# A hybrid encoder layer on one core: the far stretch's stores on GpSimd's queue, eight tiles for the last value chunks, vectors and memory loaded elsewhere

## The chip, the cores and the metric

The kernel runs on one core of a Trainium2 chip. The metric is the device time of one execution in microseconds (us), smaller is better. A core has TensorE (PE in the profile; PEld is its weight load), VectorE (DVE), ScalarE (ACT), GpSimd (POOL) and SyncE (SP). A transfer is issued by an engine: it stands in that engine's queue in program order, behind whatever that engine waits for, and then runs on the core's 16 DMA engines.

## The reference

One transformer layer on x of 2048 rows by 1024 columns, with 256 rows of memory:

```
h = x + W_out [ DilatedSWA(q,k,v) || ConformerConv(u) ],  (q,k,v,u) = RMSNorm(x) W_in
h = h + CrossAttn(RMSNorm(h), RMSNorm(mem))
h = h + SqReLU-MLP(RMSNorm(h)),   then a last RMSNorm
```

DilatedSWA is attention over three banded patterns (dilation 1, 4 and 16), whose three outputs are combined for each head by a softmax over their log-denominators. The convolution has 31 taps. The cross attention's keys and values are products of the 256 memory rows with w_xk and w_xv; the kernel multiplies the values further with w_xo (a quarter of the heads at a time) before it uses them.

## The kernel before, in words

Every large product is made of three matmuls: both factors are split into a high and a low part, and `mm3` (L263, L264, L265) adds high*high, low*high and high*low. So each weight chunk is loaded (a tile `raw`), its high part is cast by ACT (`whi`, L254), and its low part is a subtraction on DVE or POOL (`wlo`, L255; `lwlo`, L221).

The order of the program is written as Python generators that are woven into each other (`weave`), with helpers that pin a stream behind an engine's last instruction (`pinned`, `behind`), and a scheduler in the tile framework then lays the rows out for each engine. `dma` (L57) issues on SP's queue unless a queue is named. Tiles of one tag are buffers that are taken in turn: a writer of a tile waits until the reader of what lay there before is done.

By the trace, the stages are these. **Start** (0 to some 140 us): `setup` (L154) loads seven gain vectors and the convolution's weights `cwn` from ACT's queue, transposes them on PE into the bank `pvec` and makes `gv`, `cw` and `gmix`; `xprep` (L388 to L408) loads four blocks of x (`xn`), sums squares on ACT (`junk`, L375), transposes on PE (`xt`, L400), scales on DVE (`xv`, L405) and splits on ACT and POOL (`xh`, `xl`); `glu_first` is the first projection. `memory` (L414) loads and normalises the memory rows behind `xprep` 3. **Projections** to some 420 us. **Far stretch** (420 to 690): attention of the first quarter of rows, and woven into it the rest of the gated projections and the class `Matrices`: `proj` (keys and values of the memory), `turn` (transposed w_xq chunks, `xqt`, L523), `score` (`pa`, `ea`). All of these write results to scratch in DRAM on SP's queue: `pscr` (`kscr`/`vscr`<-`ve`), `uscr`, `ascr`. SP's queue carries the attention's own loads too (`k`, `qh`, `ql`, `v`, and `ld`, which is read back from `oscr`).

`combine` (L1061) joins the three patterns for two heads: it loads `ld` (SP), takes a minimum `csm` on DVE (L1081, L1082), works on POOL (L1083 to L1109) to `cat`, which PE transposes (`catT`, L1117). Its `yield`s say how many attention units lie between the steps.

**Backs** (690 to 746): `Matrices.back(i)` for i = 24 to 31 multiplies values with a chunk of w_xo (`raw_m24` to `raw_m31`, 512 KB each): for each i, two banks `pb` of six matmuls of 512 columns, each emptied by ACT into a tile `eb` (L563, through two tiles of the tag `ve`) and stored to `bscr` on SP. The chunks have two tiles `raw`, loaded two ahead on POOL's queue; `load_cat` puts 14 transfers of 256 KB (`cath`, `catl`) on SP just before. **w_out** and the rest (MLP and so on) run from 746 to the end; its first chunks `raw_o` are loaded by `ahead`.

Of the kernel before, what the change touches and what calls it, by code (L numbers as in the profile page):

```python
# [10 lines left out]
F32 = mybir.dt.float32  # L11
# [10 lines left out]
P = 128  # L22
# [25 lines left out]
def hybrid_layer(ctx, tc, A, out):  # L48
# [103 lines left out]
    cst.tile([P, 8], F32, name="lpad")  # L152
    lin = ExitStack()
    def setup():  # L154
        vecs, cwn = t2("vecs", F32, (64, P)), t2("cwn", F32, (32, DCONV))
        DVE.memset(vecs, 0.0)
        DVE.memset(cwn, 0.0)
        for nm, key in (("norm_mix_g", "mix"), ("norm_x_g", "x"), ("norm_mlp_g", "mlp"),
                        ("conv_b", "conv_b"), ("conv_ln_g", "ln_g"), ("conv_ln_b", "ln_b")):
            v = A[nm][0].rearrange("(k p) -> k p", p=P)  # L160
            dma(vecs[GV[key]:GV[key] + v.shape[0], :], v, nc.scalar)
        dma(vecs[GV["final"]:GV["final"] + 8, :], A["norm_final_g"].rearrange("(k p) -> k p", p=P), nc.scalar)
        dma(cwn[0:CW, :], A["conv_w"][0], nc.scalar)
        pv = ps("c", "pvec")
        PE.transpose(pv[:, 0:64], vecs, ident[0:64, 0:64])
        for c in range(4):
            PE.transpose(pv[:, 64 + 32 * c:96 + 32 * c], cwn[:, c * P:(c + 1) * P], ident[0:32, 0:32])
        ACT.copy(gv, pv[:, 0:64])
        ACT.activation(cw.rearrange("p a b -> p (a b)"), pv[:, 64:192], AF.Copy, scale=0.5)
# [11 lines left out]
        DVE.tensor_scalar(gmix, g8, top_[:, 4:5], None, op0=ALU.mult)  # L181

    def pow2_scale(c, inv, v, t, bits=0):

# [259 lines left out]
    class Matrices:  # L444
# [6 lines left out]
            self.split(0)  # L451

        def load(self, i):
            if i >= 32:
                return
            raw = wp.tile([P, 8, P] if i < 24 else [P, 2, 512], F32, tag="raw", name=f"raw_m{i}", bufs=2)
            if i < 24:
                src = wcols((w_xk, w_xv, w_xq)[i // KC], i % KC * P)
            else:
                h, nh = divmod(i - 24, 2)  # L460
                src = w_xo[256 * h:256 * h + 256, 512 * nh:512 * nh + 512].rearrange("(e p) m -> p e m", p=P)
            dma(raw, src, nc.gpsimd)
            self.ring[i] = raw
# [26 lines left out]
        def proj(self, i):  # L490
            mq = self.mq
            x, j = "kv"[i // KC], i % KC
            self.load(i + 2)
            wh, wl = self.ring.pop(i)
            pt = ps("mm", f"px{x}{j}")[:, 0:NMEM]
            for k in range(KC):
                mm3(pt, wh[:, k, :], wl[:, k, :], mq[k // 4][:, k % 4, :], mq[2 + k // 4][:, k % 4, :],
                    k == 0, k == KC - 1)
                if k == 1 and i + 1 < 16:
                    self.split(i + 1)  # L500
                if k % 2 and k < KC - 1:
# [3 lines left out]
            ACT.copy(t[0], pt)  # L505
            DVE.tensor_tensor(t[1], pt, f(t[0]), op=ALU.subtract)
            for q in range(2):
                dma(f(pscr[x][q, j]), f(t[q]))
            if i == 15:
                self.kt = [self.gather("k", h) for h in range(XH)]  # L510
                self.vt = []
            yield
# [19 lines left out]
        def score(self, h):  # L532
            kt, wt = self.kt, self.wt
            for k2 in range(4):
                pt = ps("mm", f"pa{h}{k2}")
                for q in range(2):
                    k = 2 * k2 + q
                    for e in range(2):
# [3 lines left out]
                e3 = ev.rearrange("p (q m) -> p q m", q=2)  # L542
                DVE.tensor_tensor(e3, pt.rearrange("p (q m) -> p q m", q=2),
                                  self.rbm.unsqueeze(1).to_broadcast([P, 2, NMEM]), op=ALU.mult)
                dma(ascr[h // 2, :, 2 * k2:2 * k2 + 2, h % 2, :], e3)
                if k2 == 3:
                    self.vt.append(self.gather("v", h))
                yield

        def back(self, i):  # L550
            h, nh = divmod(i - 24, 2)
            self.load(i + 2)
            wh, wl = self.ring.pop(i)
            vt = self.vt
            for mc in range(2):
                ms = slice(mc * P, (mc + 1) * P)
                pt = ps("mm", f"pb{h}{nh}{mc}")
                for e in range(2):
                    mm3(pt, vt[h][:, 0, e, ms], vt[h][:, 1, e, ms], wh[:, e], wl[:, e], e == 0, e == 1)
                if mc == 0:  # L560
                    self.split(i + 1)
                ev = f(self.pl.tile([P, 512], F32R, tag="ve", name=f"eb{h}{mc}{nh}", bufs=2))
                ACT.activation(ev, pt, AF.Copy, scale=rmem[:, mc:mc + 1])  # L563
                dma(bscr[4 * nh:4 * nh + 4, :, 2 * h + mc, :].rearrange("m p c -> p m c"),
                    ev.rearrange("p (m c) -> p m c", c=P))
                yield

    def linear(wh, wl, n):
# [31 lines left out]
    def glu(c, ns, fine=False):  # L600
# [4 lines left out]
        def unit(x, c0):  # L605
# [10 lines left out]
            for n in ns:  # L616
# [7 lines left out]
                else:  # L624
                    u = t2(f"u{c}_{n}")
                    last["dve"] = DVE.scalar_tensor_tensor(u, sig[n], 1.0, pt, op0=ALU.add, op1=ALU.mult)
                    dma(uscr[c][:, 15 + 512 * n:15 + 512 * (n + 1)], u)
                yield

        return unit("g", 3 * DATT + DCONV + c * P), unit("a", 3 * DATT + c * P)  # L630
# [271 lines left out]
    with ExitStack() as st:  # L902
# [7 lines left out]
        next(x1)  # L910
        next(four)
        next(four)
        next(x0)
        for _ in range(3):
            behind("sumsq", four)
        drain(x0)
        for _ in range(3):
            behind("x0_3", four)
        behind("x0_5", x1)
# [371 lines left out]
    with ExitStack() as st:  # L1291
# [6 lines left out]
        def filler():  # L1298
# [10 lines left out]
            mats.split(24)  # L1309
            yield from gated  # L1310

        rest = pinned(filler(), "pe")
        for _ in range(30):
            next(rest)
# [28 lines left out]
        def backs():  # L1343
            for i in range(24, 32):
                yield from mats.back(i)
            yield from pipeline(ahead(0), ahead(1))

        weave(pinned(backs(), "pe"), (first, 0.55))


    banks.update(mm=(0, 1, 2), O=(7,))
# [635 lines left out]
```

## Time and profile before

| | us |
|---|---|
| three runs: median, lowest, highest | 2821.86, 2818.76, 2829.14 |
| the profiled execution | 2827.31 |
| its span in the trace | 2825.5 |
| PE busy, DVE busy, ACT busy, POOL busy | 2697.4, 1898.2, 1272.6, 525.7 |

A row of a timeline shows the start, the duration, the engine, the line, the operation with the tile written and the tiles read, and in square brackets how long the engine had been idle and who released it. "issue" there means that the engine waited for nothing that the profile shows. A row of the waits shows engine, line, releaser, total us, times and the longest. A row of a window shows its length, then each engine's busy time with its number of instructions, the granted PE clock, the share of the DMA engines and GB/s.

### The profile page before, as it was taken

The numbers are of one execution on the slowest core, as the hardware profiler recorded it, in microseconds if no ns is written. First come the engines' busy times: TensorE is split into PE (matmuls) and PEld (weight loads), VectorE is DVE, ScalarE is ACT, GpSimd is POOL, SyncE is SP. The second block draws the span as 40 slices with busy tenths as digits, with TensorE's granted clock in tenths as the row PEclk, the third lists the DMA queues.
The fourth block names the chain that finished last, engine by engine and source line by source line (L and its number), as shares of the span: only waits on it lengthen the run. The fifth ranks groups of instructions, "written<-read, shape, count | busy, mean of one in ns | idle before, by whom it ended". The sixth has DMA issues, their size and how long they took to land.

```text
span 2825.5 us, 40587 instructions
## 1 busy us (share of the span) xinstructions
PE 2697.4 (95%) x14783; PEld 2075.6 (73%) x14783; DVE 1898.2 (67%) x3475; ACT 1272.6 (45%) x2171; POOL 525.7 (19%) x716
## 2 busy tenths in 40 slices
PE   6999999988899999999999999999999999999998
PEld 3544447775687787788788888887887788878887
DVE  4468826654589876668987478766475776566765
ACT  5742216644444434434554444454344444444434
POOL 4454402321002122300211201121010122100000
PEclk9999999999899999999999999999999999999999
DMA  8765547876834666776457867774534554584553
GB/s 257 204 179 117 137 133 194 256 209 190 239 114 157 214 212 211 243 226 214 144 170 227 267 190 223 239 236 141 175 122 131 182 191 156 181 292 155 166 183 104
DMA packets 484257, 535.69 MB, mean 190 GB/s; under 512 B 98021, under 2 KB 357721, under 8 KB 484056
## 3 DMA queue, kind: packets, MB, share of 16 engines
q1 hardware_dynamic: 452176, 427.76, 50.8%
q0 software_dynamic: 30032, 101.99, 10.2%
q10 hardware_dynamic: 1848, 3.33, 0.3%
q8 instruction: 116, 1.90, 0.3%
q14 instruction: 85, 0.70, 0.1%
HBM read 384.46 MB, written 148.52 MB: 189 GB/s over the span
## 4 chain that ended last, share of the span: by engine, by line
PE 69%; DMA 9%; issue 8%; DVE 6%; ACT 4%; POOL 2%; SPq 1%; ACTq 0%; POOLq 0%; DVEq 0%
PE b L1685 7%; PE dn L263 4%; PE dn L264 4%; PE dn L265 4%; PE up L263 3%; PE up L265 3%; PE up L264 3%; PE lin L263 2%; PE lin L265 2%; PE lin L264 2%; PE pt L978 2%; PE s L1170 2%; SPq L57 1%; PE x L264 1%; PE x L263 1%
## 5 line engine op out<-in xcount | busy, mean ns | idle before, releaser
L280 DVE SCALAR_TENSOR_TENSOR cacc<-cu,cwu,cacc 128x512 f32<-128x512 f32 x480 | 393.3, 821 | 6.5
L972 ACT ACTIVATE sm<-sm,o 128x256 f32<-128x256 f32 (+1 forms) x384 | 160.4, 467 | 115.2 <-DVE o L971 114.8
L263 PE MATMUL up<-mh,whi_u 128*128 128x512 f32 x512 | 204.0, 399 | 0.0
L263 PE MATMUL dn<-hhh,whi_d 128*128 128x512 f32 x512 | 201.6, 404 | 1.9 <-ACT hhh L1522 1.9
L264 PE MATMUL dn<-hhl,whi_d 128*128 128x512 f32 x512 | 199.9, 393 | 0.8 <-DVE hhl L1523 0.8
L265 PE MATMUL up<-mh,wlo_u 128*128 128x512 f32 x512 | 200.1, 391 | 0.0
L264 PE MATMUL up<-ml,whi_u 128*128 128x512 f32 x512 | 199.8, 390 | 0.0
L265 PE MATMUL dn<-hhh,wlo_d 128*128 128x512 f32 x512 | 199.0, 392 | 0.0
L971 DVE CUSTOM_DVE_ANT_0 sm<-s,mask 128x256 f32<-128x256 f32 (+1 forms) x384 | 127.2, 375 | 58.8 <-PE s L1170 33.1
L982 DVE TENSOR_TENSOR pl<-pt,ph 128x512 f16<-128x512 f32 x160 | 109.7, 686 | 49.4 <-ACT ph L981 49.0
L1537 DVE TENSOR_TENSOR h<-h,dn 128x512 f32<-128x512 f32 x128 | 86.3, 684 | 70.1 <-PE dn L265 69.5
L241 POOL TENSOR_TENSOR nr<-st_v,mhalf 128x4 f32<-128x4 f32 x12 | 13.5, 1124 | 638.7 <-DVE st_v L237 638.7
L981 ACT CAST ph<-pt 128x512 f16<-128x512 f32 x160 | 92.6, 579 | 82.5 <-PE pt L978 81.5
L265 PEld LDWEIGHTS up<-mh,wlo_u 128*128 128x128 f32 x512 | 96.2, 188 | 20.4
L265 PEld LDWEIGHTS dn<-hhh,wlo_d 128*128 128x128 f32 x512 | 96.2, 188 | 20.1
L264 PEld LDWEIGHTS dn<-hhl,whi_d 128*128 128x128 f32 x512 | 96.4, 188 | 19.1 <-DVE hhl L1523 1.4
L263 PEld LDWEIGHTS dn<-hhh,whi_d 128*128 128x128 f32 x512 | 95.5, 188 | 20.2 <-ACT hhh L1522 2.8
L264 PEld LDWEIGHTS up<-ml,whi_u 128*128 128x128 f32 x512 | 96.4, 188 | 18.5
L263 PEld LDWEIGHTS up<-mh,whi_u 128*128 128x128 f32 x512 | 96.2, 188 | 18.6
L263 PE MATMUL x<-pth,whi_b 128*128 128x512 f32 x256 | 100.9, 400 | 2.4 <-ACT xp L1446 1.5
L263 PE MATMUL o<-cath,whi_o 128*128 128x512 f32 x256 | 101.9, 399 | 0.7 <-DVE h L1402 0.7
L263 PE MATMUL xs<-whi_a,yh 128*128 128x512 f32 x256 | 102.4, 401 | 0.0
(608 smaller groups left out, 7933.5 us busy)
## 6 DMA issues: line engine op xcount, KB each, us to landing
raw_u<-in_w_up_dram SPq DMA_DIRECT2D x64, 512.0 KB
raw_d<-in_w_down_dram SPq DMA_DIRECT2D x64, 512.0 KB
k<-kscr SPq DMA_DIRECT2D x32, 640.0 KB
raw_o<-in_w_out_dram SPq DMA_DIRECT2D x32, 512.0 KB
raw_a<-ascr SPq DMA_DIRECT2D x32, 512.0 KB
raw_b<-bscr SPq DMA_DIRECT2D x32, 512.0 KB
lou<-wlo_u POOLq DMA_DIRECT2D x32, 512.0 KB, 5.6
lod<-wlo_d POOLq DMA_DIRECT2D x32, 512.0 KB, 5.7
```

The lines of the kernel that those rows point to most:

```text
L263: PE.matmul(o, lh, rh, start=first, stop=False)
L264: PE.matmul(o, lh, rl, start=False, stop=False)
L265: last["pe"] = PE.matmul(o, ll, rh, start=False, stop=end)
L280: DVE.scalar_tensor_tensor(acc, u[:, t:t + 512], cwu[:, c, t:t + 1], acc, op0=ALU.mult, op1=ALU.add)
L971: last["dve"] = DVE.tensor_tensor_reduce(dst, so, mask[:, 256 * m:256 * m + nk], 1.0, 3e38, ALU.add, ALU.min, mn)
L972: last["act"] = ACT.activation(dst, dst, AF.Exp, bias=mn, scale=-1.0)
L978: last["pe"] = PE.transpose(pt[:, j, :], sm[:, j, :], ident)
L981: ACT.copy(ph, pt)
L982: DVE.tensor_tensor(pl, pt, ph, op=ALU.subtract)
L1170: last["pe"] = PE.matmul(o, q_[x][:, qs], kv, start=x == 0, stop=x == 1)
L1537: last["dve"] = DVE.tensor_tensor(hs[m], hs[m], pt, op=ALU.add)
L1685: PE.matmul(o, w[i][:, k, :], Y[b][q][k], start=first and k + x == 0, stop=k == 3 and x == 2, skip_group_check=not first)
```

## The change

Seven edits.

1. `setup` issues the seven vectors from POOL instead of ACT; `cwn` goes into a generator `conv_weights` of its own (transfer on POOL, transposes and copy later).
2. At the start two more steps of `four` (the first weights' sums of squares) come ahead of the rest of x, and one step instead of three behind `sumsq`; `conv_weights` ends behind `x0_3`.
3. The stores to `pscr`, `uscr` (of the later gated units) and `ascr` go from SP to POOL.
4. `back` writes `eb` into eight tiles z0 to z7 instead of two, stores to `bscr` from POOL, and the chunks 26 to 29 have tiles of their own (`rb26` to `rb29`, a pool opened behind the far stretch), loaded together before the backs; 30 and 31 take the two old tiles, six ahead. `ahead` loads on POOL.
5. `memory`'s first step (its loads) comes between `xprep` 2 and 3.
6. In `combine` for the first quarter `ld` comes one unit later (two for the first three pairs of heads).
7. `backs` is defined earlier and woven inside a block that holds the new pool.

On POOL, at the end of the far stretch, the rows before were these (`ce`, `csm`, `cat` and `ld` are `combine`'s tiles of the third pair of heads; `vt` are the values):

```order
L57 DMA vt3_7197<-vscr_114 128x2x256 x2
L57 DMA raw_m26_7786<-in_w_xo_dram 128x2x512
L57 DMA raw_m27_7822<-in_w_xo_dram 128x2x512
L1083 TENSOR_TENSOR ce02_7305<-csm02_7304,o0_02_5889 128x8
...
L1109 TENSOR_TENSOR cat02_7408<-cat02_7408,ld02_7065 128x512 x2
L57 DMA raw_m28_7870<-in_w_xo_dram 128x2x512
L57 DMA raw_m29_7906<-in_w_xo_dram 128x2x512
```

The same place on POOL after the change:

```order
L57 DMA ascr_110<-ea33_7195 128x2x256
L57 DMA raw_m30_7798<-in_w_xo_dram 128x2x512
L57 DMA raw_m31_7834<-in_w_xo_dram 128x2x512
L1100 TENSOR_TENSOR ce02_7393<-csm02_7392,o0_02_5890 128x8
...
L1126 TENSOR_TENSOR cat02_7503<-cat02_7503,ld02_7179 128x512 x2
L57 DMA uscr3_73<-u3_2_7586 128x512
L57 DMA uscr3_73<-u3_3_7723 128x512
L57 DMA bscr_111<-eb000_7811 128x4x128
L57 DMA bscr_111<-eb010_7821 128x4x128
L57 DMA raw_m26_7772<-in_w_xo_dram 128x2x512
L57 DMA raw_m27_7774<-in_w_xo_dram 128x2x512
L57 DMA raw_m28_7776<-in_w_xo_dram 128x2x512
```

Chunks 30 and 31 have moved ahead of the combine, and 26 to 29 behind the stores of the first two `eb` (`eb000` and `eb010`, both of chunk 24), which wait for ACT.

On DVE, in the second pair's combine, before (`sm` is an attention unit's scores, `wlo_m18` the low part of a w_xq chunk):

```order
L971 ISA sm_6195,o1_02_6193<-s_6194,mask_3652 128x256
L971 ISA o1_02_6193 128x1
L1081 TENSOR_TENSOR csm01_6234<-ld01_5996 128x8
L1082 TENSOR_TENSOR csm01_6234<-csm01_6234,o0_01_4866 128x8
L1052 COPY o3_42_6025<-opt3_6220 128x4x65
L526 TENSOR_TENSOR wlo_m18_6185<-xqt180_6186,whi_m18_6184 128x512
```

After:

```order
L987 ISA o1_02_6194 128x1
L1068 COPY o3_42_6023<-opt3_6221 128x4x65
L534 TENSOR_TENSOR wlo_m18_6186<-xqt180_6187,whi_m18_6185 128x512
...
L534 TENSOR_TENSOR wlo_m19_6238<-xqt191_6246,whi_m19_6237 128x512
L998 TENSOR_TENSOR pl_6278<-pt_6272,ph_6277 128x512
L987 ISA sm_6300,o0_02_5890<-s_6299,mask_3653 128x256
...
L1098 TENSOR_TENSOR csm01_6337<-ld01_6073 128x8
```

`csm01` has moved 15 rows back, behind the four `wlo_m` of chunks 18 and 19 and two of the `pl`.

The diff, without the unchanged part of the moved functions:

```diff
-            dma(vecs[GV[key]:GV[key] + v.shape[0], :], v, nc.scalar)
+            dma(vecs[GV[key]:GV[key] + v.shape[0], :], v, nc.gpsimd)
...
-        dma(cwn[0:CW, :], A["conv_w"][0], nc.scalar)
...
+    def conv_weights():
+        cwn = t2("cwn", F32, (32, DCONV))
+        DVE.memset(cwn, 0.0)
+        dma(cwn[0:CW, :], A["conv_w"][0], nc.gpsimd)
+        yield
+        pv = ps("c", "pcw")
+        for c in range(4):
+            PE.transpose(pv[:, 32 * c:32 * c + 32], cwn[:, c * P:(c + 1) * P], ident[0:32, 0:32])
+        ACT.activation(cw.rearrange("p a b -> p (a b)"), pv[:, 0:P], AF.Copy, scale=0.5)
...
         def load(self, i):
-            if i >= 32:
+            if i >= 32 or i in self.ring:
                 return
-            raw = wp.tile([P, 8, P] if i < 24 else [P, 2, 512], F32, tag="raw", name=f"raw_m{i}", bufs=2)
+            if 25 < i < 30:
+                raw = self.bl.tile([P, 2, 512], F32, tag=f"rb{i}", name=f"raw_m{i}")
+            else:
+                raw = wp.tile([P, 8, P] if i < 24 else [P, 2, 512], F32, tag="raw", name=f"raw_m{i}", bufs=2)
...
-                dma(f(pscr[x][q, j]), f(t[q]))
+                dma(f(pscr[x][q, j]), f(t[q]), nc.gpsimd)
...
-                dma(ascr[h // 2, :, 2 * k2:2 * k2 + 2, h % 2, :], e3)
+                dma(ascr[h // 2, :, 2 * k2:2 * k2 + 2, h % 2, :], e3, nc.gpsimd)
...
         def back(self, i):
-            self.load(i + 2)
+            if i < 26:
+                self.load(i + 6)
...
-                ev = f(self.pl.tile([P, 512], F32R, tag="ve", name=f"eb{h}{mc}{nh}", bufs=2))
+                ev = zp.tile([P, 512], F32, tag=f"z{(2 * i + mc) % 8}", name=f"eb{h}{mc}{nh}")
...
-                    ev.rearrange("p (m c) -> p m c", c=P))
+                    ev.rearrange("p (m c) -> p m c", c=P), nc.gpsimd)
...
-                    dma(uscr[c][:, 15 + 512 * n:15 + 512 * (n + 1)], u)
+                    dma(uscr[c][:, 15 + 512 * n:15 + 512 * (n + 1)], u, nc.gpsimd if fine else None)
...
+        next(four)
+        next(four)
+        cwt = conv_weights()
+        next(cwt)
         next(x0)
-        for _ in range(3):
-            behind("sumsq", four)
+        behind("sumsq", four)
         drain(x0)
+        with ExitStack() as st0:
+            after(st0, "x0_3")
+            drain(cwt)
...
-        later = pinned(chain(xprep(sp, 2), xprep(sp, 3), memory(sp)), "x1_7")
+        mem = memory(sp)
+        later = pinned(chain(xprep(sp, 2), islice(mem, 1), xprep(sp, 3), mem), "x1_7")
...
     def combine(p, pr, o0):
-        if p:
+        yield
+        if p == 0 and pr < 3:
             yield
...
     def ahead(m):
-        dma(raw, wcols(w_out, m * P))
+        dma(raw, wcols(w_out, m * P), nc.gpsimd)
...
-        load_cat(0, 0)
-        load_cat(0, 1)
-        weave(pinned(backs(), "pe"), (first, 0.55))
+        with ExitStack() as st1:
+            mats.bl = pool("back_w", stack=st1)
+            for i in range(26, 30):
+                mats.load(i)
+            load_cat(0, 0)
+            load_cat(0, 1)
+            weave(pinned(backs(), "pe"), (first, 0.55))
```

More of the change, by code (lines that the diff above doesn't have):

```diff
@@ L154, in setup @@
     def setup():
-        vecs, cwn = t2("vecs", F32, (64, P)), t2("cwn", F32, (32, DCONV))
+        vecs = t2("vecs", F32, (64, P))
         DVE.memset(vecs, 0.0)
-        DVE.memset(cwn, 0.0)
         for nm, key in (("norm_mix_g", "mix"), ("norm_x_g", "x"), ("norm_mlp_g", "mlp"),
@@ L160, in setup @@
             v = A[nm][0].rearrange("(k p) -> k p", p=P)
-            dma(vecs[GV[key]:GV[key] + v.shape[0], :], v, nc.scalar)
-        dma(vecs[GV["final"]:GV["final"] + 8, :], A["norm_final_g"].rearrange("(k p) -> k p", p=P), nc.scalar)
-        dma(cwn[0:CW, :], A["conv_w"][0], nc.scalar)
+            dma(vecs[GV[key]:GV[key] + v.shape[0], :], v, nc.gpsimd)
+        dma(vecs[GV["final"]:GV["final"] + 8, :], A["norm_final_g"].rearrange("(k p) -> k p", p=P), nc.gpsimd)
         pv = ps("c", "pvec")
         PE.transpose(pv[:, 0:64], vecs, ident[0:64, 0:64])
-        for c in range(4):
-            PE.transpose(pv[:, 64 + 32 * c:96 + 32 * c], cwn[:, c * P:(c + 1) * P], ident[0:32, 0:32])
         ACT.copy(gv, pv[:, 0:64])
-        ACT.activation(cw.rearrange("p a b -> p (a b)"), pv[:, 64:192], AF.Copy, scale=0.5)
         g8 = gv[:, GV["mix"]:GV["mix"] + 8]
@@ L1310, in filler, with backs @@
             yield from gated
+        def backs():
+            for i in range(24, 32):
+                yield from mats.back(i)
+            yield from pipeline(ahead(0), ahead(1))
         rest = pinned(filler(), "pe")
@@ L1339, in hybrid_layer @@
         xp_ = pool("post_x", stack=dense)
-        load_cat(0, 0)
-        load_cat(0, 1)
[L1343 to L1346, printed above, removed]
-        weave(pinned(backs(), "pe"), (first, 0.55))
+        with ExitStack() as st1:
[5 more added lines that the diff above has]
+            weave(pinned(backs(), "pe"), (first, 0.55))
     banks.update(mm=(0, 1, 2), O=(7,))
```

## The prediction

> **What bounds the kernel.** I read the busy shares first, then what PE waited for, then the timelines of the places named there.
>
> ```profile
> PE 2697.4 (95%) x14783; PEld 2075.6 (73%) x14783; DVE 1898.2 (67%) x3475; ACT 1272.6 (45%) x2171; POOL 525.7 (19%) x716
> ```
>
> PE is busy for 2697.4 of a span of 2825.5 us, so 128.1 us of idle PE is all that an edit without fewer matmuls can win, beside matmuls that run at half rate after a long idle time. The change takes no matmul away. So the question is which idle times it touches.
>
> ```profile
> PE pb L263 <- ACT eb L563: 21.2, 3, 14.5
> PE xt L400 <- DMA xn<-in_x_dram: 9.0, 4, 5.6
> PE opt L988 <- DVE pl L982: 7.2, 3, 5.1
> PE xqt L523 <- issue: 6.2, 1, 6.2
> ...
> PE mt L429 <- issue: 5.1, 2, 4.7
> ```
>
> The longest, 21.2 us in three waits, is in the backs. `opt` and `xqt` are in the far stretch, `xt` at the start, `mt` in the memory's step. Each belongs to one edit; I take them in order of time.
>
> **Start: 5 us gained.**
>
> ```profile
> 7.98 1.28 ACT L375 ACT_TABLE_LOAD   x1 [7.98 <-DMA vecs<-in_conv_ln_b_dram]
> 11.08 0.69 PE L400 MATMUL xt<-ident,xn 128*128 128x128 f32 x2 [1.57 <-DMA xn<-in_x_dram]
> 15.44 0.21 ACT L168 COPY gv<-pvec 128x64 f32<-128x64 f32 x1 [3.94 <-PE pvec L167]
> 17.57 0.23 DVE L181 TENSOR_SCALAR gmix<-gv,gtop 128x8 f32<-128x8 f32 x1
> 19.36 1.04 ACT L202 ACTIVATE sqj_g<-lraw_g 128x1024 bf16<-128x1024 f32 x1
> 21.80 1.15 ACT L219 ACTIVATE lraw_g<-lraw_g,wscl 128x1024 f32<-128x1024 f32 x1 [1.31 <-DVE sqv_g L189]
> 24.54 1.41 DVE L405 SCALAR_TENSOR_TENSOR xv<-xt,gmix,rbs 128x512 f32<-128x512 f32 x2 [2.52 <-ACT rbs L395]
> ...
> 29.14 1.10 POOL L57 DMA_DIRECT2D xn<-in_x_dram  x2
> ```
>
> ACT does nothing until 7.98, since eight transfers stand ahead of its table load, and again waits 3.94 for `pvec`. Its eight `junk` are over at 19.36, though x was there by about 12 (PE's last early `xt` began at 11.08). Without the issues and with `gv` behind the `junk`, these end at about 12.8; the scaling and the cast of the first weights (1.15, and about the 1.04 of `sqj_g`, which is as large) come next, so `gv` falls at about 15.4, `gmix` 2.4 later (15.44 to 17.80) at 17.8, and the first `xv` at about 18.0 for 24.54: 6.5 us. Of this 1.1 goes back, as `cwn`'s issue now stands on POOL ahead of the first `xl` (1.10 us for two such issues). I take 5. Nothing is left of it if weights and x, which are not loaded sooner, set the pace again before the projections do; all 6.5 stay if `cwn` is hidden. Bounds 0 and 6.5.
>
> **Memory: 1 us gained.**
>
> ```profile
> 149.45 4.70 ACT L793 CAST lwhi_qr<-lraw_qr 128x512 f16<-128x512 f32 x2
> 158.01 1.93 PE L429 MATMUL mt<-ident,mn 128*128 128x128 f32 x8 [4.72 <-issue]
> ```
>
> Only the loads move, and they had landed long before 158. ACT is held by a weight's split from 149.45 to 154.15, and `mt`'s banks, which ACT and DVE empty, come free behind it. That stays, some rows away. Bounds 0 and 5.1, nearer to nothing.
>
> **Far stretch: 12 us gained.**
>
> ```profile
> 574.75 0.59 SPq L57 DMA_DIRECT2D ld<-oscr  x1
> 583.10 0.17 DVE L1081 TENSOR_TENSOR csm<-ld 128x8 f32<-128x8 f32 x1 [5.99 <-DMA v<-vtok]
> 584.52 1.09 PE L523 MATMUL xqt<-ident,raw_m 128*128 128x128 f32 x4 [6.23 <-issue]
> 586.45 0.87 PE L523 MATMUL xqt<-ident,raw_m 128*128 128x128 f32 x3 [0.84 <-DVE wlo_m L526]
> 593.56 0.20 DVE L1100 RECIPROCAL csm<-csm 128x8 f32<-128x8 f32 x1
> 661.65 0.17 DVE L1081 TENSOR_TENSOR csm<-ld 128x8 f32<-128x8 f32 x1 [7.95 <-DMA ld<-oscr]
> 663.02 0.20 PE L988 MATMUL opt<-v,pl 128*128 128x65 f16 x1 [5.13 <-DVE pl L982]
> ```
>
> DVE runs in order. At 583.10 and 661.65 a `csm` of 0.17 us makes it stand 5.99 and 7.95 us for `ld`, and PE stands behind it 6.23 and 0.84, then 5.13: 12.2 us. The second half of `ld` was issued at 574.75 and landed with the `csm`, 8.3 us later. The order moves this `csm` back by 15 rows of DVE, to where a `RECIPROCAL` stood at 593.56, about ten us on. The `ld` stands on SP behind the same `v` and `ql`, with no store ahead that waits. So `ld` is there and both waits go; the third pair is moved alike. What is late next is `cat`, on POOL, as POOL takes on 81 rows more by the order; its readers come later by as much. I take 12 of 12.2. Bounds: 0, if the next wait on DVE is as long (the slowest landing of the `raw_m`, quoted below, is 12.0), and 17, if both waits also cost a restart at half rate, 2.4 each as worked out below.
>
> **Backs: 13 us gained.**
>
> ```profile
> 693.61 0.69 ACT L563 ACTIVATE eb<-pb,rmem 128x512 f32<-128x512 f32 x1 [0.70 <-PE pb L265]
> 694.20 1.04 ACT L254 CAST whi_m<-raw_m 128x1024 fp32r<-128x1024 f32 x1
> 705.86 1.85 SPq L57 DMA_DIRECT2D bscr<-eb  x2
> 711.81 1.45 ACT L563 ACTIVATE eb<-pb,rmem 128x512 f32<-128x512 f32 x2 [13.42 <-DMA bscr<-eb]
> 712.54 0.79 PE L263 MATMUL pb<-whi_m,vt 128*128 128x512 f32 x1 [14.48 <-ACT eb L563]
> 717.83 0.29 PE L1170 MATMUL s<-k,qh 128*128 128x256 f16 x1
> 718.21 0.48 PE L263 MATMUL pb<-whi_m,vt 128*128 128x512 f32 x1
> 721.07 0.60 PE L978 MATMUL pt<-ident,sm 128*128 128x128 f32 x4
> 732.30 0.79 PE L263 MATMUL pb<-whi_m,vt 128*128 128x512 f32 x1 [3.94 <-ACT eb L563]
> 743.14 0.50 PE L263 MATMUL pb<-whi_m,vt 128*128 128x512 f32 x1 [2.76 <-ACT eb L563]
> ...
> DMA to landing us min/median/max: 4.5/6.3/12.0
> ```
>
> Both `eb` of chunk 24 were done by 694.30, but their stores left SP at 705.86, behind 14 `cath`/`catl`. The third `eb` waited for a tile until 711.81 and PE until 712.54. Idle: 14.48 + 3.94 + 2.76 = 21.2. Then twelve matmuls took 5.29 (712.54 to 717.83) where the next twelve took 2.86 (718.21 to 721.07): 2.4 more, and 2.4 again after 732.30, whose first row also shows 0.79. In all 26.0.
>
> With eight tiles and stores on POOL, no `eb` waits for these stores. What is late next is chunk 26: before, it was loaded early, on POOL; now its issue stands behind the stores of both `eb` of chunk 24. 694.3 + 0.36 (a store's issue) + 0.72 (a load's) = 695.4; plus 6.3 to landing and 1.04 for its cast is 702.7. PE, which was done at 698.06, waits 4.7, and 2.4 go at half rate: 7.1. Then PE meets earlier what was hidden: the next `v`, and w_out's chunks. I put one landing, 6.3, on that: 26.0 - 7.1 - 6.3 = 12.6, so 13. Bounds: landing 12.0 gives an idle time of 10.4, 12.8 with the restart, and 12.0 for the next wait: 26.0 - 24.8 = 1. Landing 4.5 and no other wait: 26.0 - 5.3 = 21.
>
> The Trainium skill, in "DMA: Bandwidth & Descriptors", section "Anatomy of one DMA — SWDGE (gpsimd) path", has a fit of 2.0 us plus bytes over 436e3, so 3.2 us by estimate for 512 KB. The trace shows 4.5 at the least. By the fit the wait for chunk 26 would be 3 us shorter and the sum 34.
>
> **Sum.** 5 + 1 + 12 + 13 = 31 us off the profiled execution's 2827.3: 2796. The median of the runs, 2821.9, is 5.4 below that execution, so 2791 against it. The stages after 746 are the same work; I count them at nothing, as PE is the bound there.
>
> **Rivals.**
>
> ```profile
> 690.00:750.00 60.00, 38.82 (x229) 29.91 (x227) 22.29 (x61) 28.30 (x48) 2.91 (x4) 0.80 0.84 250
> 705.00:710.00 5.00, 0.00 (x0) 0.00 (x0) 0.00 (x0) 0.00 (x0) 0.00 (x0) 0.50 1.05 397
> 517.48 0.20 POOL L1083 TENSOR_TENSOR ce<-csm,o 128x8 f32<-128x8 f32 x1 [1.98 <-DVE csm L1082]
> 529.08 2.47 POOL L1109 TENSOR_TENSOR cat<-cat,ld 128x512 f32<-128x512 f32 x2
> L505 ACT CAST ve<-pxv x8: 361/363/372, 489.9 to 554.7; 128x256 fp32r<-128x256 f32 x8
> ```
>
> *The same DMA engines.* Moving an issue moves no bytes. While PE stood still (705 to 710) the engines were full at 397 GB/s, and over the backs' 60 us their share was 0.84; squeezed into 47 us the same work would be a share of 1.07. Then the four chunks and the `cath` land late whoever issues them. The backs give 26.0 - 12.8 - 8 = 5, the far stretch 5 (`ld` still takes over 8 us), the start 5: 15 gained, 2812, and 2807 against the median. For it speaks the full window, against it that `cath` now waits for a later `ld` on SP, so the chunks go first. Chance 0.18. The Trainium skill states this rule in the same page, section "Issuing engines are not separate DMA queues": transfers from all issuers run on the same 16 engines, and several issuers save only the time of issuing. The trace agrees as far as the window at 397 GB/s, but the store at 705.86 also shows a queue in which order, not bandwidth, cost 11 us.
>
> *POOL becomes the queue that is waited for (slower).* A store behind a combine on POOL waits for `csm` (up to 7.95, the DVE's wait) and for the combine (517.48 to 531.55, 14.1), then 6.3 to landing: 28.4 us. Two `ve` tiles at 9.3 us each (seven steps in 489.9 to 554.7) cover 18.5. Beyond 18.5 PE stops: 9.9 + 2.4 for the restart at each of three combines is 37 lost; `ea` has more tiles, so that is the far end. With the start's 5 and the backs' 13 kept, 19 are lost: 2846, 2841 against the median. Against it: `csm` moves so that its wait should go. Chance 0.07.
>
> *All of it is kept.* Upper bounds with no new wait: 6.5 + 5 + 16 + 20 = 47, so 2780, 2775 against the median. Chance 0.12.
>
> *It does not do what it says*: the order lets chunk 26 leave late, the start is given back and the far wait only moves, 0 to 10 gained, 2817 against the median. Chance 0.08.
>
> **How the numbers follow.** The forecast has 0.55. Its own range, from 24 to 38 gained, is 2784 to 2798. No more than 2 in 10 should be left out: 2768 is below the third rival's time, 2815 takes in the first. Half a per cent, 14.1 us, is about what a measurement of this kernel can tell from no change. Faster by more than that: 0.53 of the forecast, 0.10 of the first rival (its time lies at the bound), 0.12 of the third: 0.75. Slower: 0.07. Within: 0.18.
>
> **What would show it.** In the new profile the wait of `pb` for `eb` is gone, and one of 3 to 10 us for `whi_m` or `raw_m` of chunk 26 stands in its place, at about 690 to 705. The idle time before `csm` is below 2 us for the second and third pair. The first `xv` starts at 17 to 20. If instead DVE stands at `csm` for 6 us or more, or POOL's stores stand long behind `cat` while DVE or ACT wait for `ve` or `ea`, the far stretch's term is wrong; if PE waits 10 us or more in the backs for `raw_m`, `cath` or `raw_o` with the engines full, the first rival is right.

## The result, and the profile after

Seven runs of the changed kernel have a median of 2801.03 us (2797.16 to 2812.21), seven of the kernel before 2822.13 (2818.76 to 2829.14). The ratio is 0.9933, with an interval of 0.9913 to 0.9952: 0.7 per cent faster. The profiled execution took 2799.84 us (span 2798.1), 27.5 below the one of before, and so gained more than the medians, which are 21.1 apart.

The page of the changed kernel, and PE's longest waits (engine, line, releaser, total us, times, longest):

```profile
PE 2692.8 (96%) x14783; PEld 2072.3 (74%) x14783; DVE 1905.7 (68%) x3475; ACT 1271.6 (45%) x2171; POOL 583.6 (21%) x798
```

```profile
PE s L1187 <- DVE o L987: 8.5, 3, 7.6
PE xt L405 <- DMA xn<-in_x_dram: 8.4, 4, 5.3
PE opt L1004 <- DVE pl L998: 6.2, 5, 2.9
PE xqt L531 <- DVE wlo_m L534: 6.1, 5, 1.8
PE pgain L254 <- DVE gtop L168: 5.5, 1, 5.5
...
PE o L268 <- ACT whi_o L259: 4.5, 2, 2.4
...
PE pb L268 <- ACT whi_m L259: 3.4, 1, 3.4
```

PE's idle time fell from 128.1 us to 2798.1 - 2692.8 = 105.3. The wait of `pb` for `eb` (21.2 us) is gone, and so are the 6.2 of `xqt` and the 5.1 of `mt`. New are `s` behind DVE's `o` (8.5), `pgain` (5.5), `o` behind `whi_o` (4.5) and `pb` behind `whi_m` (3.4).

Waits do not tell where the end moved, since a wait that goes in one place may come back in another. So I set the start of each PE matmul of one trace against the same matmul of the other (same tile, same number in its row) and took the median of the differences within 8 us of a mark. This is the **lead** over the kernel before. The marks are times of the kernel before; the column "after" is the changed kernel's profiled execution, the others are variants that are told below.

| mark, us | after | u_start | u_mem | u_comb | u_queue | u_back |
|---|---|---|---|---|---|---|
| 100 | 4.6 | 0.3 | 5.5 | 5.8 | 5.9 | 5.2 |
| 130 | 9.9 | 5.9 | 4.2 | 10.4 | 10.4 | 10.0 |
| 170 | 16.4 | 12.3 | 3.8 | 16.9 | 16.6 | 16.5 |
| 410 | 16.2 | 11.6 | 6.5 | 16.2 | 16.7 | 16.1 |
| 570 | 17.4 | 12.4 | 7.1 | 13.6 | 17.2 | 13.2 |
| 690 | 25.9 | 19.7 | 19.0 | 8.4 | 32.1 | 26.2 |
| 800 | 26.8 | 22.4 | 17.8 | 8.2 | 33.2 | 25.6 |

For the changed kernel the steps are: start 4 to 5 us, memory 12, far stretch 9.5, backs and the beginning of w_out 1. In a second profiled execution of the same kernel (experiment 6) they are 5.5, 10.6, 4.2 and 0.6, so the far stretch's step is the uncertain one. Between 690 and 800 the lead rises to 44 at 740 and falls again, because PE runs the backs' matmuls ahead of attention's, which it then owes. Behind 800 the work is the same, and single executions differ there by some us either way.

### The profile page after: what moved, and what is told of

The parts are those of the page before. It is cut to its first block, busy times and chain, and to the rows that moved or that the text cites. A ratio compares the mean times of both kernels' runs of the same rounds, so it can differ in the third digit from the quotient of the medians.

```text
span 2798.1 us, 40584 instructions
## 1 busy us (share of the span) xinstructions
PE 2692.8 (96%) x14783; PEld 2072.3 (74%) x14783; DVE 1905.7 (68%) x3475; ACT 1271.6 (45%) x2171; POOL 583.6 (21%) x798
## 4 chain that ended last, share of the span: by engine, by line
PE 68%; issue 9%; DMA 8%; DVE 7%; ACT 3%; POOL 3%; SPq 2%; POOLq 0%; ACTq 0%; DVEq 0%
PE b L1705 8%; PE dn L268 4%; PE dn L269 4%; PE dn L270 4%; PE up L268 3%; PE up L270 3%; PE up L269 3%; SPq L57 2%; PE lin L269 2%; PE lin L270 2%; PE lin L268 2%; PE pt L994 2%; PE s L1187 2%; PE x L269 1%; PE x L268 1%
## 5 line engine op out<-in xcount | busy, mean ns | idle before, releaser
L987 DVE CUSTOM_DVE_ANT_0 sm<-s,mask 128x256 f32<-128x256 f32 (+1 forms) x384 | 126.9, 374 | 45.3 <-DMA oscr<-o 16.9
L269 PEld LDWEIGHTS dn<-hhl,whi_d 128*128 128x128 f32 x512 | 96.8, 189 | 19.7 <-DVE hhl L1543 1.8
L270 PE MATMUL o<-cath,wlo_o 128*128 128x512 f32 x256 | 102.2, 401 | 1.5 <-DVE wlo_o L260 1.5
```

The lines of the kernel that those rows point to most:

```text
L269: PE.matmul(o, lh, rl, start=False, stop=False)
L270: last["pe"] = PE.matmul(o, ll, rh, start=False, stop=end)
L987: last["dve"] = DVE.tensor_tensor_reduce(dst, so, mask[:, 256 * m:256 * m + nk], 1.0, 3e38, ALU.add, ALU.min, mn)
```

## The experiments

Times are ratios to the kernel before, run beside each variant on the same chip, with their intervals. Where a stretch is measured, "far" runs from the first `s` to the first `pb` (before 255.9 us, changed 246.4) and "backs" from the first `pb` to the first `x<-pth`, which takes in w_out (before 159.2, changed 158.3). Each of these lengths is from one profiled execution.

**1. Memory's loads back behind `xprep` 3 (u_mem).**

```diff
-        mem = memory(sp)
-        later = pinned(chain(xprep(sp, 2), islice(mem, 1), xprep(sp, 3), mem), "x1_7")
+        later = pinned(chain(xprep(sp, 2), xprep(sp, 3), memory(sp)), "x1_7")
```

> The changed kernel with memory's loads again behind xprep 3. In the changed kernel's trace PE's lead over the kernel before grows from about 4 us at 100 to 16 us at 170, as two waits (3.0 at 117.84 for xt, 4.7 at 158.01 for mt) are gone. Theory M (the place of memory's loads makes the lead): without it the lead at 170 is 4 to 6 us, and the time 9 to 13 us above the changed kernel's. Rival S (the lighter start makes it, by shifting everything): the lead at 170 stays 13 us or more and the time is within 4 us of the changed kernel's.

Measured: 0.9960 (0.9945 to 0.9975), and a lead of 3.8 us at 170. Theory M holds for the lead; in time the ratio is 0.0027 above the changed kernel's 0.9933, 7.6 us, and so a little below the 9 to 13 that were expected. The timelines show how. Before, ACT, DVE and PE in turn (start, duration, engine, line, operation, and in brackets the idle time before it):

```profile
106.68 0.63 ACT L375 ACTIVATE junk<-mn 128x512 bf16<-128x512 f32 x1 [2.81 <-DMA mn<-in_mem_dram]
...
111.26 1.57 DVE L383 TENSOR_TENSOR ssm<-ssm 128x2 f32<-128x2 f32 x1 [5.24 <-ACT junk L375]
...
117.84 1.09 PE L400 MATMUL xt<-ident,xn 128*128 128x128 f32 x4 [3.00 <-issue]
```

After, DVE at the same sum:

```profile
107.87 0.14 DVE L388 TENSOR_TENSOR ssm<-ssm 128x2 f32<-128x2 f32 x1
```

The memory rows `mn` came late, ACT stood for them, DVE stood 5.24 us for ACT's sum, and PE's next `xt` had no free bank. "issue" in PE's row hides this, as the bank's release is not named. With the loads ahead, DVE no longer waits at that row. The second wait, 4.72 before `mt`, went along with it: ACT's split of `lwhi_qr` still takes 4.77 us (from 135.30), and the last `mt` waits 0.34; why it waits less was not followed further.

The two waits are 7.7 us, and the lead grew by 12. The windows from 100 to 170 (length, busy time of PE, PEld, DVE, ACT, POOL, granted clock, DMA share, GB/s), before and after, show the rest:

```profile
100.00:170.00 70.00, 61.43 (x296) 31.96 (x294) 38.65 (x66) 41.20 (x64) 30.68 (x33) 0.93 0.75 188
100.00:170.00 70.00, 68.68 (x351) 35.00 (x350) 41.58 (x67) 43.95 (x67) 36.12 (x37) 1.00 0.77 196
```

PE stood still for 8.6 us of the 70 before and for 1.3 after, and the granted clock rose from 0.93 to 1.00, which over 70 us is worth about 5 us more (an estimate: 0.07 of 70).

**2. The old start (u_start).** The seven vectors and `cwn` on ACT's queue in `setup`, and the old order of `four`.

```diff
-            dma(vecs[GV[key]:GV[key] + v.shape[0], :], v, nc.gpsimd)
+            dma(vecs[GV[key]:GV[key] + v.shape[0], :], v, nc.scalar)
...
-        next(four)
-        next(four)
-        cwt = conv_weights()
-        next(cwt)
         next(x0)
-        behind("sumsq", four)
+        for _ in range(3):
+            behind("sumsq", four)
```

> The changed kernel with the old setup (vectors and cwn on ACT's queue, cwn in setup) and the old start order; memory's loads stay where the change put them. Theory M: the lead at 60 is about 0 for 4 to 5, but it still grows by 10 to 12 us between 100 and 170, so the time is 4 to 5 us above the changed kernel's. Rival S: the lead at 170 is below 6 us and the time 12 to 16 us above.

Measured: lead 0.3 at 100 and 12.3 at 170, so the start is worth 4 us and the memory's 12 stands without it (theory M). The ratio, 0.9925 (0.9896 to 0.9955), can't tell 4 us from nothing.

**3. Combine's old yields (u_comb).**

```diff
-        yield
-        if p == 0 and pr < 3:
+        if p:
             yield
```

> The changed kernel with combine's old yields, stores still on POOL. Theory Y (the later ld and csm make the far stretch's lead of 9.5 us): the waits before csm of 6 and 8 us come back, and the time is 8 to 11 us above the changed kernel's. Rival Q (SP's queue without stores makes it, since ld leaves earlier): waits before csm stay below 3 us and the time is within 3 us.

Measured: 0.9981 (0.9966 to 0.9996); far 262.8 us, longer than before the change. DVE's waits at `csm` in this kernel:

```profile
573.52 0.17 DVE L1097 TENSOR_TENSOR csm<-ld 128x8 f32<-128x8 f32 x1 [10.05 <-issue]
...
652.58 0.17 DVE L1097 TENSOR_TENSOR csm<-ld 128x8 f32<-128x8 f32 x1 [9.18 <-issue]
```

They were 5.99 and 7.95 before. Theory Y holds: the later yields make the gain. More than that: with the stores on POOL and without the yields these waits are longer than before the change, and 8 us of the lead are lost.

**4. The three stores back on SP, yields kept (u_queue).**

```diff
-                dma(f(pscr[x][q, j]), f(t[q]), nc.gpsimd)
+                dma(f(pscr[x][q, j]), f(t[q]))
...
-                dma(ascr[h // 2, :, 2 * k2:2 * k2 + 2, h % 2, :], e3, nc.gpsimd)
+                dma(ascr[h // 2, :, 2 * k2:2 * k2 + 2, h % 2, :], e3)
...
-                    dma(uscr[c][:, 15 + 512 * n:15 + 512 * (n + 1)], u, nc.gpsimd if fine else None)
+                    dma(uscr[c][:, 15 + 512 * n:15 + 512 * (n + 1)], u)
```

> The changed kernel with the stores to pscr, uscr and ascr back on SP's queue, combine's later yields kept. Theory Y (the later yields make the far stretch's lead): the time is within 3 us of the changed kernel's and no wait before csm is over 3 us. Rival Q (the queue makes it): 6 to 10 us above, with csm waiting 5 us or more.

Measured: 0.9897 (0.9873 to 0.9921), far 240.4 us, and waits of 0 and 2.16 us before the second and third `csm`. The waits are as theory Y said, and rival Q is wrong. But the ratio is 5 to 10 us better than the changed kernel's two (0.9933 here, 0.9916 in experiment 6), a sign that neither theory had; the intervals overlap. SP's `ld` and `v` and DVE's `csm` in the changed kernel:

```profile
557.63 1.25 SPq L57 DMA_DIRECT2D ld<-oscr  x2
558.98 7.43 SPq L57 DMA_DIRECT2D v<-vtok  x5
...
571.74 0.17 DVE L1098 TENSOR_TENSOR csm<-ld 128x8 f32<-128x8 f32 x1 [3.81 <-DMA ld<-oscr]
...
617.91 18.60 SPq L57 DMA_DIRECT2D v<-vtok  x12
636.61 0.54 SPq L57 DMA_DIRECT2D ld<-oscr  x1
...
642.72 0.17 DVE L1098 TENSOR_TENSOR csm<-ld 128x8 f32<-128x8 f32 x1 [5.92 <-DMA ld<-oscr]
```

and POOL's stores to `ascr` there, 256 KB each:

```profile
553.48 0.71 POOL L57 DMA_DIRECT2D ascr<-ea  x1 [7.77 <-DVE ea L551]
554.90 0.72 POOL L57 DMA_DIRECT2D ascr<-ea  x1 [0.71 <-DVE o L987]
556.95 0.72 POOL L57 DMA_DIRECT2D ascr<-ea  x1 [1.33 <-DVE ea L551]
```

The same rows with the stores on SP:

```profile
557.00 1.08 SPq L57 DMA_DIRECT2D ld<-oscr  x2
558.18 5.25 SPq L57 DMA_DIRECT2D v<-vtok  x5
563.57 4.70 SPq L57 DMA_DIRECT2D ascr<-ea  x3
...
568.09 0.17 DVE L1098 TENSOR_TENSOR csm<-ld 128x8 f32<-128x8 f32 x1
...
615.61 8.86 SPq L57 DMA_DIRECT2D v<-vtok  x7
625.37 3.31 SPq L57 DMA_DIRECT2D v<-vtok  x5
628.78 1.71 SPq L57 DMA_DIRECT2D ascr<-ea  x2
630.88 0.36 SPq L57 DMA_DIRECT2D ld<-oscr  x1
...
636.97 0.17 DVE L1098 TENSOR_TENSOR csm<-ld 128x8 f32<-128x8 f32 x1 [2.16 <-DMA ld<-oscr]
```

With fewer rows of its own SP got through its `v` more slowly: five took 7.43 instead of 5.25 us, twelve 18.60 instead of 8.86 + 3.31 = 12.17. The first `ld` left at the same time (557.63 and 557.00), but DVE had to stand until 571.74, where it had not waited at all at 568.09; the second left 5.7 us later, 2.0 of which the first wait had cost. What differs is when the stores leave. On POOL an `ascr` store left 0.3 to 1.0 us after DVE had made its `ea`, so four of them (553.48 to 559.97) ran beside the `v` and the `ld`: 247 and 245 GB/s from 550 to 555 and 555 to 560, where it was 164 and 184 with the stores on SP. On SP the same four stood in the queue behind the `v` and the `ld` and left from 563.57 on, some ten us after their `ea`; around 620 to 635 the four were held back likewise, two of them behind the `ld` and all behind the `v`. So SP's row went faster where the stores were held back behind the loads that DVE waits for. Whether a store on POOL's queue slows SP's transfers beyond that was not tested: no run has the stores on POOL at the later time.

**5. Only the `ascr` stores back on SP (ascr_sp).**

```diff
-                dma(ascr[h // 2, :, 2 * k2:2 * k2 + 2, h % 2, :], e3, nc.gpsimd)
+                dma(ascr[h // 2, :, 2 * k2:2 * k2 + 2, h % 2, :], e3)
```

> The changed kernel with the stores to ascr alone back on SP, those to pscr and uscr still on POOL. With all three back on SP the far stretch, from the first s to the first pb, took 240 to 242 us, with all on POOL 246 to 251, and the difference arose at two combines, around 572 and 643, while ascr and uscr are stored. Theory A (the ascr stores on POOL slow SP's v transfers, behind which ld stands): the far stretch takes 240 to 243 us here, DVE waits 0 to 3 us before each csm, ratio 0.988 to 0.9905. Rival (uscr's or pscr's share, or any store on POOL): 245 us or more, DVE waits 4 us or more before csm, ratio 0.991 to 0.994.

Measured: 0.9896 (0.9877 to 0.9916), far 243.2 us, and DVE waits 1.73 and 3.49 us before the second and third `csm`. That is close to theory A and a little short of it: most of the gain of experiment 4 is there with `ascr` alone. Its stores leave 11 to 14 us after their `ea` at these two combines, as in experiment 4. What is left, 3 us, is within what single executions differ by (experiment 6), so it is not shown that the other stores cost something.

**6. The changed kernel once more (after_again)**, with no edit, beside q_cat and q_bytes below.

> The changed kernel itself once more, beside the next ones. Theory Q2 (the stores on POOL cost time, as the kernel with them back on SP was faster): its ratio to the kernel before is 0.992 to 0.995, some 0.3 per cent worse than the 0.9897 of the kernel whose pscr, uscr and ascr stores are on SP. Rival (that ratio was a lucky sample): 0.989 to 0.991 here too.

Measured: 0.9916 (0.9900 to 0.9932), between the two theories. Far is 250.5 us here, 246.4 in the first profile, so the same program varies by 4 us in this stretch. Four variants (u_mem, u_start, u_back and x_o1) have the rows of PE, POOL and SP in the same order as the changed kernel in this stretch; all six executions lie between 243.2 and 250.5, mean 247.1. With the three stores on SP there are two, 240.4 and 242.1 (u_queue and q_cat), and with `ascr` alone 243.2. The kernel before and the two of experiment 8, alike up to the backs, have 252.0 to 258.4, mean 255.4. So the change gains some 8 us in this stretch, and the stores on SP some 6 more. The three ratios with `ascr` on SP, 0.9897, 0.9904 and 0.9896, stand beside 0.9933 and 0.9916, and their intervals overlap in part.

**7. The old `back()` (u_back)**: two `eb` tiles, `bscr` on SP, chunks loaded two ahead, `ahead` on SP.

```diff
-                ev = zp.tile([P, 512], F32, tag=f"z{(2 * i + mc) % 8}", name=f"eb{h}{mc}{nh}")
+                ev = f(self.pl.tile([P, 512], F32R, tag="ve", name=f"eb{h}{mc}{nh}", bufs=2))
...
-                    ev.rearrange("p (m c) -> p m c", c=P), nc.gpsimd)
+                    ev.rearrange("p (m c) -> p m c", c=P))
...
-            mats.bl = pool("back_w", stack=st1)
-            for i in range(26, 30):
-                mats.load(i)
```

> The changed kernel with the old back(): two eb tiles, bscr stores on SP, chunks loaded two ahead, w_out's first chunks loaded on SP. My ledger gives the new back() a lead of only 1 us between 690 and 850, as PE's wait for eb of 21.2 us is replaced by waits for chunk 26 (4.2), for DVE behind a store of o (7.6) and for w_out's chunks (5.5). Theory: the wait of 14 us for eb is back and the time is 0 to 3 us above the changed kernel's. Rival (the prediction's term, 13 us): 10 us or more above.

Measured: 0.9921 (0.9890 to 0.9951), backs 159.8 us: as fast as the changed kernel within the intervals. `eb` has PE wait again, but in four parts (3.28, 7.25, 2.52 and 2.26 us), not 14 at once.

**8. Parts of the new `back()` alone in the kernel before.** b_tiles has the eight tiles, b_queue the `bscr` stores on POOL:

```diff
-                ev = f(self.pl.tile([P, 512], F32R, tag="ve", name=f"eb{h}{mc}{nh}", bufs=2))
+                ev = zp.tile([P, 512], F32, tag=f"z{(2 * i + mc) % 8}", name=f"eb{h}{mc}{nh}")
```

```diff
-                    ev.rearrange("p (m c) -> p m c", c=P))
+                    ev.rearrange("p (m c) -> p m c", c=P), nc.gpsimd)
```

> The kernel before with eight tiles z0 to z7 for eb and nothing else changed: bscr still on SP behind cath and catl, chunks 26 and 27 loaded early on POOL as before. Theory T (the tiles were the whole of the wait for eb): the waits for eb (21.2 us) go, also chunk 26's of 4.2, but a wait of 5 to 10 us for DVE behind the store of o comes, and w_out's chunks wait: 3 to 8 us below the kernel before. Rival (the stores' place on SP binds even with eight tiles): waits for eb of 5 us or more stay, and the time is within 2 us of the kernel before.

> The kernel before with the bscr stores on POOL's queue, two tiles for eb as before. Theory (order on SP held the stores for 11 us): the first eb wait falls from 14.5 to about 6 to 8 us (issue plus a landing), as POOL issues at once, but every later pair of eb waits for a landing too: waits for eb 12 to 20 us in all, time within 4 us below the kernel before. Rival: waits for eb below 5 us and 10 us or more below.

Measured: 0.9990 (0.9972 to 1.0007) and 1.0000 (0.9982 to 1.0018); backs 156.7 and 159.0 us. In b_tiles no wait for `eb` was left, but `pb` now waited 5.90 us for a chunk, `s` 2.91 for DVE, and the lead of 15.1 at 720 was 0.8 at 800. In b_queue the waits for `eb` were 11.5 us in six parts, the longest 3.50 where 6 to 8 was expected. In b_tiles the waits for `eb` ended as theory T said; its gain of 3 to 8 us is not shown. One edit removes the wait for `eb` and the other halves it, and the end does not move clear of noise.

**9. What binds the backs: order or bytes?** First the one late store of `o` from ACT's queue (x_o1), since DVE stood for it in the changed kernel. Rows of ACT, PE, SP and DVE there:

```profile
674.51 1.04 ACT L259 CAST whi_m<-raw_m 128x1024 fp32r<-128x1024 f32 x1 [2.37 <-DMA raw_m<-in_w_xo_dram]
675.61 0.49 PE L268 MATMUL pb<-whi_m,vt 128*128 128x512 f32 x1 [3.42 <-ACT whi_m L259]
...
694.88 2.35 SPq L57 DMA_DIRECT2D oscr<-o  x1
...
705.63 0.42 DVE L987 CUSTOM_DVE_ANT_0 sm<-s,mask 128x256 f32<-128x256 f32 x1 [9.61 <-DMA oscr<-o]
...
707.15 0.37 PE L1187 MATMUL s<-k,qh 128*128 128x256 f16 x1 [7.57 <-DVE o L987]
710.21 0.79 PE L268 MATMUL o<-cath,whi_o 128*128 128x512 f32 x1 [2.05 <-ACT whi_o L259]
```

```diff
-                    os_.rearrange("p b h e -> p b (h e)"), None if far else nc.scalar)
+                    os_.rearrange("p b h e -> p b (h e)"), None if far and pr < 3 else nc.scalar)
```

> The changed kernel with one store, that of the last pair's o of pattern 1, on ACT's queue instead of behind cath, catl, k and v on SP's. Theory O (order on SP: this store's landing at 705.6 is what DVE waits 9.6 us for, and PE 7.6 behind it): the store leaves 5 to 8 us earlier, PE's wait before s falls below 2 us, and the time is 4 to 8 us below the changed kernel's. Rival B (the DMA engines are full, or k, v and w_out's chunks are late by as much): another wait of 5 us or more stands within 20 us behind it, and the time is within 2 us.

Measured: 0.9938 (0.9914 to 0.9963), backs 159.8 us. The store left 3.4 us earlier, counted from the first `pb`, not 5 to 8. The wait of 7.57 us is gone and another of the same size is there, as rival B said. PE in x_o1:

```profile
719.29 0.22 PE L1002 MATMUL opt<-v,ph 128*128 128x65 f16 x1 [7.77 <-DMA v<-vtok]
```

Then `cath` and `catl` were taken off SP's queue (q_cat, with experiment 4's stores on SP):

```diff
-                dma(f(cats[p][q, k]), f(src[k][:, 512 * p:512 * (p + 1)]))
+                dma(f(cats[p][q, k]), f(src[k][:, 512 * p:512 * (p + 1)]), None if p else nc.gpsimd)
```

> Stores to pscr, uscr, ascr back on SP, and the 14 cath and catl transfers before the backs on POOL's queue instead of SP's. In the changed kernel PE needs 158 us from the first pb to the first x<-pth, 159 before the change. Theory E (the 16 DMA engines bind there: 375 to 404 GB/s at a share of 1.0 from 680 to 700): moving the issues moves no bytes, the length stays 155 to 160 us. Rival O (the order on SP binds, as v, k and the store of o stand behind cath and catl): the wait of 7 to 10 us for DVE behind that store goes and the length falls to 148 to 153 us, the time by 5 to 10 us.

Measured: 0.9904 (0.9886 to 0.9922), backs 159.5 us, the length of theory E. On SP, free of `cath`, four `v` of 65 KB still took 6.35 us, the `ld` behind them was late, and DVE stood 16.94 us for it. Rows of SP, DVE and PE in q_cat, and its windows:

```profile
686.40 6.35 SPq L57 DMA_DIRECT2D v<-vtok  x4
...
694.57 0.53 SPq L57 DMA_DIRECT2D ld<-oscr  x1
...
700.50 0.17 DVE L1098 TENSOR_TENSOR csm<-ld 128x8 f32<-128x8 f32 x1 [16.94 <-DMA ld<-oscr]
702.26 0.79 PE L268 MATMUL pb<-whi_m,vt 128*128 128x512 f32 x1 [14.20 <-ACT eb L572]
...
690.00:695.00 5.00, 0.00 (x0) 0.00 (x0) 0.00 (x0) 0.00 (x0) 0.00 (x0) 0.56 0.52 149
695.00:700.00 5.00, 0.00 (x0) 0.00 (x0) 0.00 (x0) 0.00 (x0) 0.00 (x0) 0.50 0.74 226
```

This run is no clean sign for theory E. PE's wait of 14.20 us hangs on that `ld`: the `eb` that PE waits for stands on ACT behind the combine's `ce`, and `ce` waits for `csm`. While PE stood, the engines' share was 0.52 and 0.74, so they were not full. A new wait of order has the place of the old one.

**10. Fewer bytes in the backs (q_bytes)**, with experiment 4's stores on SP. Twelve of the sixteen `bscr` stores, 3 MB, are left out; other data are stored to those places in the far stretch, so the output is not the reference's.

```diff
-                dma(bscr[4 * nh:4 * nh + 4, :, 2 * h + mc, :].rearrange("m p c -> p m c"),
-                    ev.rearrange("p (m c) -> p m c", c=P), nc.gpsimd)
+                if i < 26:
+                    dma(bscr[4 * nh:4 * nh + 4, :, 2 * h + mc, :].rearrange("m p c -> p m c"),
+                        ev.rearrange("p (m c) -> p m c", c=P), nc.gpsimd)
```

> Stores to pscr, uscr, ascr back on SP; and of the 16 bscr stores of the backs 12 (3 MB) are left out, with other data (ea) stored to those places in the far stretch instead, so the output is not the reference's. Theory E (bytes bind in the backs): 3 MB at 400 GB/s is 7.5 us, so the length from the first pb to the first x<-pth falls from 158 to 149 to 153 us. Rival O (order on SP binds): these stores are on POOL, so the length stays 156 to 159 us.

Measured: 0.9862 (0.9843 to 0.9880), backs 148.1 us where u_queue, the same kernel with the stores in place, has 158.1: theory E, and a little more than its 7.5 us. The far stretch, to which the other data were moved, took 245.5 us, 5.1 more than u_queue's. Of 14 profiled executions, the kernel before among them, it is the only one whose backs do not take 156 to 161 us. The windows (length, busy time of PE, PEld, DVE, ACT, POOL, granted clock, DMA share, GB/s) of the changed kernel:

```profile
680.00:690.00 10.00, 10.00 (x64) 8.01 (x63) 5.21 (x15) 8.45 (x16) 3.67 (x6) 0.96 1.04 404
690.00:700.00 10.00, 9.59 (x66) 7.59 (x65) 3.14 (x3) 5.17 (x8) 5.55 (x7) 1.00 1.01 375
```

and of q_bytes, whose backs begin at 665.5:

```profile
675.00:685.00 10.00, 9.68 (x60) 7.96 (x61) 6.18 (x17) 8.45 (x16) 0.00 (x0) 1.00 1.03 392
685.00:695.00 10.00, 10.00 (x71) 8.04 (x70) 4.26 (x5) 6.85 (x11) 1.79 (x2) 1.00 0.94 311
```

In the changed kernel PE is busy while the engines run at their full 400 GB/s, and stands still afterwards. With 3 MB less the full time is shorter, and PE's wait at `s` for DVE is 1.93 us, where u_queue has 9.58 and the changed kernel 7.57. The whole backs of u_queue and of q_bytes:

```profile
658.40:816.54 158.14, 139.13 (x771) 110.70 (x767) 104.19 (x209) 74.73 (x131) 18.21 (x23) 0.94 0.59 185
665.52:813.62 148.10, 134.23 (x771) 107.48 (x767) 103.83 (x209) 74.50 (x131) 9.19 (x11) 0.97 0.58 176
```

Half of the ten us is idle time of PE (19.0 and 13.9), the other half goes with the granted clock, 0.94 and 0.97. Two rivals are left. The twelve stores also leave POOL's queue, and w_out's first two chunks, which stand behind some of them, left 1.5 and 2.1 us earlier than in u_queue, counted from the first `pb`; but the store of `o`, on SP, left 4.0 us earlier, and it does not stand in POOL's queue. And the scheduler laid some 30 of PE's 764 matmuls there in another order, behind the wait at `s`. So bytes are the best supported cause, not the only one possible.

## Why the prediction was right, and where it was not

The forecast was 2791 (2768 to 2815) and faster; measured are 2801.03 and faster. That is inside the range, but 3 us outside the narrower one of the forecast itself (2784 to 2798). The sum of 31 stands against 27.5 on the profiled execution and 21.1 between the medians. The terms were less right than the sum.

- **Start, 5 us: right in size.** Lead 4.6 at 100, 0.3 without the edit. The table load moved from 7.98 to 0.74 and the first `xv` from 24.54 to 19.88, not 18.0, because `gtop`'s chain ran later than I put it: PE's `pgain` waited for it until 17.28.

```profile
0.74 1.28 ACT L207 ACT_TABLE_LOAD   x1 [0.74 <-PEq L1990]
...
17.28 0.45 PE L254 MATMUL pgain<-ident,gtop 128*128 128x128 f32 x1 [5.53 <-DVE gtop L168]
...
19.88 1.41 DVE L410 SCALAR_TENSOR_TENSOR xv<-xt,gmix,rbs 128x512 f32<-128x512 f32 x2 [0.69 <-ACT rbs L400]
```

- **Memory, 1 us: 12 measured, the largest miss upwards.** The failed step is "they had landed long before 158". That is true of the row at 158, and the wrong row to look at: the loads were late at 106.68 already, and the row of 3.00 us at 117.84 that this caused was not in my part at all. "That stays, some rows away", of the wait before `mt`, failed too: 0.34 us of it is left. Even my upper bound, 5.1, was short; it also had no term for half-rate time, which I did price elsewhere and which made about 5 of the 12.
- **Far stretch, 12 us: 9.5 measured on the profiled pair, some 8 as a mean (experiment 6), by a cause that was half right.** The later `csm` is what gains (experiment 3). "So `ld` is there and both waits go" failed: 3.81 and 5.92 us are left, because SP's `v` and `ld` took longer. I had counted it as help that no store stands ahead on SP; the stores that left earlier on POOL cost some 6 us (experiments 4 to 6).
- **Backs, 13 us: 1 measured, the lower bound.** The mechanism ahead of it was right: `eb` no longer waits, and chunk 26 makes PE wait 3.42 us where I had 4.7. The failed term is "one landing, 6.3, on that" for what is late next. It measured 7.57 + 2.05 + 2.42 + 1.07 = 13.1 us of idle time. Half-rate time, of which I let only 2.4 come back, hardly shrank either: the granted clock over this stretch was 0.92 before and 0.94 after. The first rival, with 5 us for the backs, had full engines as its mechanism, which experiment 10 supports and experiment 9 leaves open. For the far stretch it had 5 us too, less than the mean of 8.
- **The slower rival** did not come. What the stores on POOL touched was SP's loads, as they left earlier.

That the sum came out close is luck: a miss of 11 in the memory's term met one of 12 in the backs.

Two rules were weighed in the prediction. The Trainium skill, "DMA: Bandwidth & Descriptors", section "Issuing engines are not separate DMA queues", says that transfers of all issuers share the same 16 engines, and that several issuers save only the time of issuing. The lengths of the backs agree: in every order of the same bytes they take 156 to 161 us. The far stretch shows what the second half of the rule leaves out, as there the choice of issuer moved the stores by some ten us, and the stretch was some 6 us longer. By the fit of the Trainium skill's same page, section "Anatomy of one DMA — SWDGE (gpsimd) path", chunk 26's load would have taken 3.2 us (an estimate); its issue ended at 670.17 and ACT's cast began at 674.51, so 4.3, and the measured figure counts.

**The better version** is the changed kernel with the `ascr` stores, or all three kinds, on SP: 0.9896 (0.9877 to 0.9916) and 0.9897 (0.9873 to 0.9921) of the kernel before. Both beat the kernel before clearly; over the changed kernel the gain is 0.2 to 0.4 per cent, which the profiles support and the intervals alone do not prove.

## What to carry to other kernels

Where a stretch keeps its length under every change of order, while the waits in it only change their names, ask for the bytes: take some out, and see if the stretch gets shorter; and look at each changed order's own trace, as a new wait of order can keep the length as well. A load that is late costs where its first reader stands in an in-order queue, not where the matmul waits that uses it; follow the wait back through each engine before you price a move of the load. And a store that nobody waits for does less harm behind the loads in a busy queue than on a free queue, where it leaves at once and runs beside them.

## What was not expected of the hardware

- A transfer queue with fewer rows became slower: five `v` on SP took 7.43 us with the 256 KB stores on POOL's queue, 5.25 with them on SP's own; twelve took 18.60 and 12.17. With the stores on SP, they stood behind these loads and left some ten us later.
- The same program's far stretch took 246.4 us in one execution and 250.5 in another. Why was not tested.
